# A hybrid encoder block on one core: x loaded and transposed in blocks of columns, and the norm's factors put into the gate results

## The chip, the cores and the metric

The kernel runs on one core of a Trainium2 chip. TensorE multiplies matrices, VectorE, ScalarE and GpSimd do elementwise work, SyncE issues most of the loads, and 16 DMA engines move the data between HBM and the core's memories. The metric is the device time of one execution in microseconds (us), less is better.

## What is computed

The reference, cut to the parts around the change (512 positions, 2048 channels, all in float32):

```python
def rms_norm(x, g):
    y = x * lax.rsqrt(jnp.mean(x * x, axis=-1, keepdims=True) + EPS)
    return y * g

def reference(x, c, w_ada, b_ada, norm_mix, w_in, ...):
    c_act = jax.nn.silu(c)
    mod = c_act @ w_ada[l] + b_ada[l]                      # 2048 -> 6 * 2048
    sh_m, sc_m, g_m, sh_f, sc_f, g_f = jnp.split(mod, 6, axis=-1)
    h = rms_norm(x, norm_mix[l]) * (1.0 + sc_m) + sh_m
    proj = h @ w_in[l]                                     # 2048 -> 512 + 1536 + 2048 + 2048
    y_s5 = s5_branch(proj[..., :512], ...)                 # two state-space scans, 32 groups
    y_fn = fnet_branch(proj[..., 512:2048])                # 2-D Fourier transform
    gate_s5 = jax.nn.sigmoid(proj[..., 2048:4096])
    gate_fn = jax.nn.sigmoid(proj[..., 4096:])
    merged = gate_s5 * (y_s5 @ w_branch_s5[l]) + gate_fn * (y_fn @ w_branch_fnet[l])
    x = x + g_m * (merged @ w_out[l])
    ...                                                    # a second norm, a SwiGLU layer, a last norm
```

## The kernel before

Every product is done with three matmuls: a weight is split into a rounded part `whi` (ScalarE, L123) and a rest `wlo` (VectorE, L124), the activations likewise into `hi` and `lo` (tiles `actA`, `actB`), and `mm3` (L206 to L208) sums three of the four products. Activations lie transposed: channel blocks k = 0 to 15 of 128 rows, 512 positions as columns.

The kernel is a list of steps. A step may have a job: a load (SyncE's queue), a preparation (the splits) and the matmuls that use it. `run_plan` walks the list: it issues loads in the order of the steps (moved forward by a job's `lead`) as long as buffers are free (five `raw`, eight `araw`, three `whi`/`wlo`), prepares up to three steps ahead, and then issues the step's own work. On TensorE and GpSimd the instructions stand in the order in which the program writes them; on VectorE and ScalarE a scheduler orders them, except that instructions marked `keep_in_program_order` stay in order among themselves. Each engine works through its own list in order.

The start needs `x` transposed (`xT`, the tile `mg`), the row factors of the norm (`rb`, from the sums of squares `xs`), and `mod[1]`, the scale, which is a product of `c` with 16.8 MB of `w_ada`. The scale comes in five blocks of 2, 4, 4, 4 and 2 channel blocks. The first is summed on TensorE (`ada_pe`, L312), the others by VectorE, one multiply-add per 128x512 piece (L283, L285, tiles `ada`), and a sum over partitions on TensorE (`ada_fin`, L329). `form_hs` then makes the scaled activations of a channel block: `s_mix` (L405), `htmp` = `xT` times `s_mix` times `rb` (L413), and its split. `start_w(k)` multiplies them with six gate tiles' weights, 18 matmuls for each k, and six accumulators stay open over k = 0 to 15.

Then six more gate tiles (n = 6 to 11) are computed, each from two weight halves, while the shift `mod[0]` (another 16.8 MB of `w_ada`) is summed in the same way. These twelve tiles are multiplied without the shift; they are stored as they are and finished later. In tile 11 `resplit` calls `form_h` behind each k: `htmp` is made again and the shift is added on the way into `hi` and `lo` (L127, L128). After its last k the pool that holds `xT` and `rb` is closed, and later tiles take its memory.

Next come `u_fn`, the 512 inputs of the S5 branch, and then 20 gate tiles, with hooks between their matmuls that build the S5 matrices in eight batches: the parameters (some 120 small operations on VectorE, recorded by `Deferred` and issued two at a time in tiles 6 to 10; they all show as L516), copies and transposes of them, loads of the tables `R` and `cn` (`s5_load`, L714 and L718) into memory that becomes free with the closed pools, `Y` on VectorE (`s5_a`, L731 to L736), and `TB` and `E` on GpSimd (L750 to L778), which TensorE transposes (L820). The rest (Fourier branch, output, SwiGLU layer) is some 2000 us of matmuls.

`sxT` is a copy of `xT` in HBM, read again much later; GpSimd issues its four stores (L935), the first instructions on its list behind the loads of S5 parameters.

## Time and profile before

| | us |
|---|---|
| median of 3 runs | 2518.16 (2514.17 to 2520.89) |
| the profiled execution | 2523.47 |
| its span, first to last instruction | 2521.7 |
| TensorE busy in the span | 2419.8 |
| VectorE busy | 1673.8 |
| ScalarE busy | 1014.5 |
| GpSimd busy | 562.4 |

The mean granted clock of TensorE is 0.977 of full speed. The span is 1.8 us shorter than the execution's own time. In the profile PE is TensorE, PEld its weight loads, DVE VectorE, ACT ScalarE, POOL GpSimd, SP SyncE, and a q behind the name is the engine's queue of DMA issues. A busy TensorE is not one at its peak, since its instructions are pipelined.

### The profile page before, as it was taken

To read this page: it belongs to the slowest core of one execution; us is meant where nothing else is said; L and a number is where in the kernel's file an instruction comes from. 1 tells how busy PE (TensorE), PEld (TensorE's weight loads), DVE (VectorE), ACT (ScalarE), POOL (GpSimd) and SP (SyncE) were. 2 spreads that over 40 slices of the span, in tenths; PEclk is the share of its full clock that TensorE was granted. 3 is DMA by queue.
4 is the path that set the end of the run, shared out by engine and by line. 5 is a ranking of instruction groups with operands and counts; after the bars stand their busy time and mean duration, and the time that the engine had idled before them with its cause. 6 is when DMAs were issued, how large, how long until landed. Compare 5 with 4: busy or idle time off the path is not lost.

```text
span 2521.7 us, 37777 instructions
## 1 busy us (share of the span) xinstructions
PE 2419.8 (96%) x14450; PEld 2147.8 (85%) x14450; DVE 1673.8 (66%) x2492; ACT 1014.5 (40%) x1420; POOL 562.4 (22%) x630
## 2 busy tenths in 40 slices
PE   6899899989999999999999999999999999999997
PEld 5787777778788888888999999999999978888886
DVE  6988677636666996668667676766667645554335
ACT  3224333333223432244555555555555522233223
POOL 1002999800002520000222222222222310010001
PEclk7899999989999999999999999999999999999998
DMA  9886645447774667763788888889888877754442
GB/s 367 287 298 129 158 137 157 140 136 242 232 238 146 199 194 234 243 218 107 174 197 193 193 200 190 199 201 197 195 197 194 213 273 244 239 167 163 148 142 90
DMA packets 440678, 496.33 MB, mean 197 GB/s; under 512 B 51104, under 2 KB 336288, under 8 KB 440496
## 3 DMA queue, kind: packets, MB, share of 16 engines
q1 hardware_dynamic: 359472, 384.68, 48.7%
q0 software_dynamic: 52736, 78.74, 17.5%
q10 hardware_dynamic: 28288, 30.49, 4.2%
q8 instruction: 113, 1.85, 0.3%
q14 instruction: 69, 0.57, 0.1%
HBM read 394.13 MB, written 40.89 MB: 173 GB/s over the span
## 4 chain that ended last, share of the span: by engine, by line
PE 73%; POOL 9%; DVE 7%; DMA 5%; issue 3%; ACT 1%; SPq 1%; ACTq 0%; DVEq 0%; POOLq 0%
PE ps_acc L206 7%; PE ps_acc L207 7%; PE ps_acc L208 7%; PE ps_acc L1498 6%; PE ps_acc L1497 6%; PE ps_acc L1499 6%; PE ps_acc L1666 3%; PE ps_acc L1667 3%; PE ps_acc L1665 3%; PE ps_accb L1499 3%; PE ps_accb L1498 3%; PE ps_accb L1497 3%; DMA raw<-in_w_in_dram 2%; DVE wlo L124 2%; PE ps_m L1499 1%
## 5 line engine op out<-in xcount | busy, mean ns | idle before, releaser
L124 DVE TENSOR_TENSOR wlo<-raw,whi 128x1024 fp32r<-128x1024 f32 (+2 forms) x264 | 323.3, 1225 | 151.5 <-ACT whi L123 144.7
L123 ACT CAST whi<-raw 128x1024 fp32r<-128x1024 f32 (+2 forms) x264 | 260.5, 988 | 401.3 <-PE ps_acc L207 180.5
L1451 POOL DMA_DIRECT2D wlo<-raw x160 | 192.3, 1202 | 895.6 <-ACT wlo L1450 569.9
L206 PE MATMUL ps_acc<-actB,whi 128*128 128x512 f32 x816 | 328.3, 402 | 0.0
L207 PE MATMUL ps_acc<-actB,whi 128*128 128x512 f32 x816 | 321.7, 394 | 0.0
L208 PE MATMUL ps_acc<-actB,wlo 128*128 128x512 f32 x816 | 321.3, 394 | 0.0
L124 DVE TENSOR_TENSOR lT<-raw,hT 128x1024 fp32r<-128x1024 f32 x160 | 195.5, 1222 | 133.7 <-ACT hT L123 133.5
L123 ACT CAST hT<-raw 128x1024 fp32r<-128x1024 f32 x160 | 167.6, 1047 | 161.6 <-issue 99.4
L124 DVE TENSOR_TENSOR actA<-ab,actA 128x512 fp32r<-128x512 f32 x88 | 61.7, 703 | 234.6 <-ACT actA L123 234.6
L1449 ACT CAST whi<-raw 128x768 fp32r<-128x768 f32 x160 | 133.2, 832 | 151.7 <-PE ps_acc L1498 144.7
L208 PEld LDWEIGHTS ps_acc<-actB,wlo 128*128 128x128 f32 x816 | 155.5, 191 | 33.8
L206 PEld LDWEIGHTS ps_acc<-actB,whi 128*128 128x128 f32 x816 | 156.3, 192 | 32.8 <-issue 2.5
L123 ACT CAST actA<-ab 128x512 fp32r<-128x512 f32 x88 | 54.7, 623 | 318.9 <-PE ps_m L1666 298.2
L207 PEld LDWEIGHTS ps_acc<-actB,whi 128*128 128x128 f32 x816 | 156.2, 191 | 30.1
L1460 DVE TENSOR_TENSOR raw<-raw 128x512 f32<-128x512 f32 x160 | 110.7, 692 | 71.0 <-DMA wlo<-raw 65.4
L1666 PE MATMUL ps_acc<-wlo,actA 128*128 128x512 f32 x352 | 137.3, 390 | 1.9 <-DVE wlo L124 1.9
L285 DVE SCALAR_TENSOR_TENSOR ada<-raw,c_s,ada 128x512 f32<-128x512 f32 x180 | 136.7, 759 | 3.4
L1665 PE MATMUL ps_acc<-whi,actA 128*128 128x512 f32 x352 | 137.6, 391 | 1.0 <-DVE ab L1509 0.9
L1667 PE MATMUL ps_acc<-whi,actA 128*128 128x512 f32 x352 | 137.0, 389 | 0.0
L1450 ACT ACTIVATE wlo<-raw 128x768 fp32r<-128x768 f32 x160 | 134.3, 840 | 0.0
L1688 POOL TENSOR_TENSOR actB<-actB 128x512 f32<-128x512 f32 x15 | 23.0, 1548 | 429.1 <-ACT fot L1686 429.1
L206 PE MATMUL ps_acc<-actA,whi 128*128 128x512 f32 x272 | 111.7, 411 | 2.4 <-ACT actA L123 2.4
(474 smaller groups left out, 7006.7 us busy)
## 6 DMA issues: line engine op xcount, KB each, us to landing
raw<-in_w_ffn_in_dram SPq DMA_DIRECT2D x168, 512.0 KB
raw<-in_w_ada_dram SPq DMA_DIRECT2D x128, 512.0 KB
wlo<-raw POOLq DMA_DIRECT2D x160, 384.0 KB, 5.6
raw<-in_w_in_dram SPq DMA_DIRECT2D x108, 512.0 KB
raw<-in_w_ffn_out_dram SPq DMA_DIRECT2D x88, 512.0 KB
araw<-in_w_ada_dram SPq DMA_DIRECT2D x64, 512.0 KB
ab<-sg SPq DMA_DIRECT2D x88, 256.0 KB
raw<-in_w_out_dram SPq DMA_DIRECT2D x32, 512.0 KB
```

What stands on the lines that cost most here:

```text
L123: A.copy(hi, src)
L124: V.tensor_tensor(out=lo, in0=src, in1=hi.bitcast(F32), op=ALU.subtract)
L206: PE.matmul(o, whi, ahi, start=start, stop=False)
L207: PE.matmul(o, whi, alo, start=False, stop=False)
L208: PE.matmul(o, wlo, ahi, start=False, stop=stop)
L1451: G.dma_start(out=lo, in_=r[:, :, 0:3], accum_op=ALU.add)
L1497: PE.matmul(o, wh[:, i, q], ah, start=first and opens, stop=False, skip_group_check=True)
L1498: PE.matmul(o, wh[:, i, q], al, start=False, stop=False, skip_group_check=True)
L1499: PE.matmul(o, wl[:, i, q], ah, start=False, stop=last, skip_group_check=True)
L1665: PE.matmul(o, gh[:, ts_], hi[:, cs], start=(k == 0), stop=False)
L1666: PE.matmul(o, gh[:, ts_], lo[:, cs], start=False, stop=False)
L1667: PE.matmul(o, gl[:, ts_], hi[:, cs], start=False, stop=(k == NF - 1))
```

## The change

- `x` is loaded in four blocks of 512 columns (all rows) instead of four blocks of rows, into `araw` buffers. The first block's load stands behind the loads of the scale's first block; the others stand among the scale's blocks 1 to 3. A block is transposed by TensorE through two `ps_m` banks, and ScalarE copies all of it to `xT` and sums the squares.
- The norm's factors are needed only later: `form_hs` takes `xT` times `s_mix` alone, `hi` in one ScalarE instruction and `lo` in one on VectorE. The results of the first twelve gate tiles are multiplied by `rb` on VectorE, where ScalarE copied them. `x_rstd` moves into the last scale block, and `rb` into another pool. `form_h` (tile 11) is as before.
- The second block of the scale stands behind both of the first gate steps, no longer ahead of the last of them.
- The S5 parameters and the four stores of `sxT` are kept in program order; the stores go to ScalarE's queue.

```diff
@@ constants, and the per-column vectors
-AHEAD = 1
...
-    pv = ps_m((P, P))
-    PE.transpose(pv, rows, ident)
-    V.tensor_copy(vec, pv)
+    def vec_columns():
+        pv = ps_m((P, P))
+        PE.transpose(pv, rows, ident)
+        V.tensor_copy(vec, pv)
@@ ada_pe: the first block of the scale
-    def ada_pe(width, then):
+    def ada_pe(width):
...
                 if q == parts - 1:
                     n = width // P
+                    vec_columns()
                     V.tensor_reduce(out=mod[1][:, 0:n], in_=pt[0], op=ALU.add, axis=mybir.AxisListType.X)
                     V.tensor_tensor(out=mod[1][:, 0:n], in0=mod[1][:, 0:n], in1=vec[:, KT:KT + n], op=ALU.add)
-                    then()
@@ the loads and transposes of x
-    xs_ = cpool.tile([P, 4, 4], F32, name="xs")
-    rb = y_pool.tile([P, S], F32, name="rb")
-
-    def x_job(t):
-        def load():
-            if t < 2:
-                r = [raw_tile([P, D // 2]) for _ in range(2)]
+    xs_ = cpool.tile([P, 7, 4], F32, name="xs")
+    rb = nat_pool.tile([P, S], F32, name="rb")
+
+    def x_step(j):
+
+        def load():
+            r = [y_pool.tile([P, 2, S], F32, tag="araw", bufs=ARAW_BUFS, name="xr") for _ in range(2)]
+            for h in range(2):
+                nc.sync.dma_start(out=r[h], in_=x[2 * h * P:2 * (h + 1) * P, j * S:(j + 1) * S].rearrange(
+                    "(t p) c -> p t c", p=P))
+            return r
+
+        def fn(r):
+            for i in range(4):
+                pt = ps_m((P, 4, P))
+                for t in range(4):
+                    PE.transpose(pt[:, t, :], r[t // 2][:, t % 2, i * P:(i + 1) * P], ident)
+                A.copy(mg[:, 4 * j + i, :], pt.rearrange("p t c -> p (t c)"))
+            if j:
+                squares(r)
             else:
...
-        def prep(r):
-            for q in range(4):
-                pt = ps_acc((P, 4, P))
-                for k in range(4):
-                    kk = (4 * q + k) % 8
-                    PE.transpose(pt[:, k, :], r[q // 2][:, kk * P:(kk + 1) * P], ident)
-                dst = mg[:, 4 * q:4 * q + 4, t * P:(t + 1) * P]
-                if q == 3:
-                    A.copy(dst, pt)
-                else:
-                    V.tensor_copy(dst, pt)
-            for h in range(2):
-                junk = ring.tile([P, D // 2], F32R, tag="whi", bufs=WH_BUFS, name="junk")
-                A.activation(out=junk, in_=r[h], func=AF.Square, accum_out=xs_[:, h, t:t + 1])
-            return None
-
-        return Job(load, prep, raw=(("raw" if t < 2 else "araw", 2),), keep=())
+                x0.append(r)
+
+        def squares(r):
+            for t in range(4):
+                junk = cpool.tile([P, S], F32, tag="tmp", bufs=3, name="junk")
+                tc.keep_in_program_order(A.activation(out=junk, in_=r[t // 2][:, t % 2, :], func=AF.Square,
+                                                      accum_out=xs_[:, j, t:t + 1]))
+
+        job = Job(load, lambda r: r, raw=(("araw", 2),), keep=(), hold=True)
+        if j == 0:
+            job.late = 2
+            return [(job, fn), (None, forms(*blocks[0])), (None, lambda _: squares(x0.pop()))]
+        return [(job, fn)]
...
@@ form_hs and gate_epi
         hi, lo = act_tile(k), act_tile(k)
-        split(hi, lo, scaled_x(k))
+        A.activation(out=hi, in_=mg[:, k, :], func=AF.Copy, scale=s_mix[:, k:k + 1])
+        V.scalar_tensor_tensor(out=lo, in0=mg[:, k, :], scalar=s_mix[:, k:k + 1], in1=hi.bitcast(F32),
+                               op0=ALU.mult, op1=ALU.subtract)
...
             if dst is sg5 and n < N_HS:
-                A.copy(s, pt)
+                V.tensor_tensor(out=s, in0=pt, in1=rb, op=ALU.mult)
@@ the steps of the start
-    start_steps = []
+    start_steps = ada_pe(blocks[0][1] * P) + x_step(0)
     for i, (k0, nk) in enumerate(blocks):
...
+        if i:
+            blk = ada_steps(1, k0 * P, nk * P, True, forms(k0, nk))
+            if i < 4:
+                blk[4:4] = x_step(i)
+            if i == 4:
+                blk.insert(1, (None, x_rstd))
+            at = len(start_steps) - (i > 1)
+            start_steps[at:at] = blk
         for k in range(k0, k0 + nk):
-            ws.append((wjob(w_in_v[:, k, G0:G0 + N_START * P]), start_w(k)))
-            ws[-1][0].lead = 3 + k - k0
-        if i == 0:
-            start_steps += [(x_job(t), nop) for t in range(4)]
-            start_steps += blk[:-1] + [(None, x_rstd)] + blk[-1:] + ws
-        else:
-            start_steps[-AHEAD:-AHEAD] = blk
-            start_steps += ws
+            start_steps.append((wjob(w_in_v[:, k, G0:G0 + N_START * P]), start_w(k)))
+            start_steps[-1][0].lead = (3 if i else 2) + k - k0
@@ Deferred.issue (the S5 parameters)
-                getattr(V, name)(*a, **kw)
+                tc.keep_in_program_order(getattr(V, name)(*a, **kw))
@@ gate tiles 7 to 10
-                nc.gpsimd.dma_start(out=sxT.rearrange("k p s -> p k s")[:, 4 * q:4 * q + 4],
-                                    in_=mg[:, 4 * q:4 * q + 4])
+                tc.keep_in_program_order(A.dma_start(
+                    out=sxT.rearrange("k p s -> p k s")[:, 4 * q:4 * q + 4], in_=mg[:, 4 * q:4 * q + 4]))
```

On SyncE's queue, at the head of the program (the columns are line, what is loaded from where, the shape, and how many in a row), before:

```order
L371 DMA raw<-in_x_dram 128x1024 x4
L371 DMA xr<-in_x_dram 128x1024 x4
L303 DMA araw<-in_w_ada_dram 128x4x256 x3
L136 DMA raw<-in_w_in_dram 128x768
L303 DMA araw<-in_w_ada_dram 128x4x256
L270 DMA araw<-in_w_ada_dram 128x2x512 x5
```

The same place in the changed kernel:

```order
L304 DMA araw<-in_w_ada_dram 128x4x256 x4
L370 DMA xr<-in_x_dram 128x2x512 x2
L135 DMA raw<-in_w_in_dram 128x768 x2
L271 DMA araw<-in_w_ada_dram 128x2x512 x4
L370 DMA xr<-in_x_dram 128x2x512 x2
```

Two loads of `x` instead of eight stand ahead of the first weights, and behind the scale's first block.

On VectorE, where tile 10 ends and the shift is added (`mod` is the shift of the last four channel blocks, `htmp` and `actA` are form_h's), before:

```order
L285 SCALAR_TENSOR_TENSOR ada<-araw,c_s,ada 128x512 x5
L124 TENSOR_TENSOR wlo<-raw,whi 128x1024
L285 SCALAR_TENSOR_TENSOR ada<-araw,c_s,ada 128x512
L124 TENSOR_TENSOR wlo<-raw,whi 128x1024
L330 TENSOR_TENSOR mod_91<-ps_m,vec 128x4
L413 SCALAR_TENSOR_TENSOR htmp<-xT,s_mix,rb 128x512
```

The same place in the changed kernel:

```order
L457 TENSOR_TENSOR sg<-ps_acc,rb 128x512
L528 CAST t_1061<-kj 64x64
L123 TENSOR_TENSOR wlo<-raw,whi 128x1024
L528 TENSOR_SCALAR t_1061<-t_1061 64x64
L331 TENSOR_TENSOR mod_88<-ps_m,vec 128x4
L528 TENSOR_TENSOR si<-si,t_1061 64x64
L528 TENSOR_SCALAR t_1062<-t_1060 64x64
L429 SCALAR_TENSOR_TENSOR htmp<-xT,s_mix,rb 128x512
L528 TENSOR_TENSOR t_1061<-t_1061,t_1062 64x64
```

The S5 parameters (L528, before L516) now reach into the sixteen `htmp`, 35 of the 123 behind the first of them; all were done ahead of these before.

On ScalarE's list, gate tiles 6 to 8 of the changed kernel (`sg` is a gate tile's result, `whi` a weight's rounded part):

```order
L122 CAST whi<-raw 128x1024
L947 DMA sxT<-xT 128x4x512
L460 DMA sg_100<-sg 128x512 x3
L122 CAST whi<-raw 128x1024 x2
L947 DMA sxT<-xT 128x4x512
```

The stores of `sxT` stand between the weights' conversions, where before GpSimd issued all four with no work ahead of them. From the first `TB` on GpSimd's list is the same in both kernels, and so are TensorE's and ScalarE's from the first table of that batch on.

## Rows read from the trace of the kernel before

**Rows 1.** Stretch: busy us of PE, PEld, DVE, ACT, POOL; clock, DMA share, GB/s.

```profile
238.00:478.00 240.00, 218.22 (x1121) 176.22 (x1119) 171.82 (x214) 79.96 (x150) 225.48 (x334) 0.96 0.54 151
478.00:2521.00 2043.00, 1994.73 (x12404) 1800.83 (x12404) 1306.88 (x1848) 856.35 (x1146) 329.09 (x280) 0.99 0.71 193
```

**Rows 2.** Who waited for whom up to 490 us: us in total, times, longest.

```profile
PE ps_m L329 <- DVE ada L285: 19.8, 4, 12.0
...
PE ps_m L820 <- POOL TB L752: 15.0, 8, 4.6
...
POOL TB L750 <- DVE Y L733: 22.4, 1, 22.4
...
SPq L714 <- DVE htmp L413: 9.5, 1, 9.5
```

**Rows 3.** The chain that ended last, 200 to 240 us: start, us, what.

```profile
204.78 0.23 PE ps_acc L206
...
212.09 1.41 DVE htmp L413 x2
...
230.77 5.32 DMA R<-in_s_b_re_dram
...
237.35 1.10 DVE Y L736
```

**Rows 4.** Busy time by stretch of the start (columns as in rows 1).

```profile
0.00:20.00 20.00, 11.90 (x85) 11.59 (x85) 10.14 (x29) 12.81 (x23) 5.98 (x15) 1.00 0.92 318
20.00:60.00 40.00, 24.79 (x104) 21.06 (x104) 29.63 (x85) 8.37 (x13) 0.68 (x1) 0.66 1.04 400
60.00:100.00 40.00, 35.89 (x153) 29.33 (x152) 38.39 (x82) 9.88 (x14) 0.00 (x0) 0.91 0.74 244
100.00:160.00 60.00, 56.29 (x245) 46.37 (x244) 57.21 (x135) 18.05 (x29) 0.00 (x0) 0.94 1.02 341
160.00:180.00 20.00, 20.00 (x98) 16.87 (x97) 18.85 (x34) 5.10 (x6) 0.00 (x0) 1.00 0.92 305
...
sum 214.00, PE 182.86 PEld 151.09 DVE 180.12 ACT 71.69 POOL 6.66; mean PE 26.12 PEld 21.58 DVE 25.73 ACT 10.24 POOL 0.95
```

**Rows 5.** Instructions in order of time: start, us, engine, line [idle before, releaser].

```profile
0.72 2.08 SPq L371 DMA_DIRECT2D raw<-in_x_dram  x4
...
17.64 3.04 POOL L935 DMA_DIRECT2D sxT<-xT  x4 [12.99 <-DVE xT L384]
...
50.66 1.87 PE L329 MATMUL ps_m<-ones,ada 128*128 128x1 f32 x8 [11.96 <-DVE ada L285]
...
190.50 0.74 DVE L413 SCALAR_TENSOR_TENSOR htmp<-xT,s_mix,rb 128x512 f32<-128x512 f32 x1
...
237.00 1.29 POOL L750 TENSOR_TENSOR TB<-Y,powr 128x512 f32<-128x512 f32 x1 [22.36 <-DVE Y L733]
```

**Rows 6.** DMA issues up to 214 us: count, size of each, us to landing.

```profile
sxT<-xT POOLq DMA_DIRECT2D x4, 1024.0 KB, 14.5
...
raw<-in_x_dram SPq DMA_DIRECT2D x4, 512.0 KB
```

**Rows 7.** Groups of instructions: count, busy us, mean ns, idle before.

```profile
L413 DVE SCALAR_TENSOR_TENSOR htmp<-xT,s_mix,rb 128x512 f32<-128x512 f32 x32 | 22.9, 746 | 0.0
...
L384 DVE COPY xT<-ps_acc 128x512 f32<-128x512 f32 x12 | 7.7, 687 | 1.7 <-PE ps_acc L379 1.7
...
L387 ACT ACTIVATE junk<-xr 128x1024 fp32r<-128x1024 f32 x4 | 4.2, 1054 | 0.0
```

**Rows 8.** VectorE's busy time in L516 alone, by stretch.

```profile
0.00:60.00 60.00, 6.90 (x42) 0.77 1.00 373
60.00:180.00 120.00, 14.07 (x81) 0.94 0.91 303
```

**Rows 9.** TensorE's busy time and granted clock around its first gate matmuls.

```profile
30.79:36.89 6.10, 5.22 (x11) 0.50 1.03 415
36.89:38.70 1.81, 1.81 (x8) 0.99 1.03 404
```

More of the change, by code (lines that the diff above doesn't have):

```diff
@@ L392, in x_rstd, with forms, fn @@
+        return [(job, fn)]
+    x0 = []
+    def forms(k0, nk):
+        def fn(_=None):
+            for k in range(k0, k0 + nk):
+                form_hs(k)
+        return fn
     def x_rstd(_):
-        v, r, t = (xs_[:, i, :] for i in (2, 3, 1))
-        V.tensor_tensor(out=v, in0=xs_[:, 0, :], in1=xs_[:, 1, :], op=ALU.add)
+        v, r, t = (xs_[:, i, :] for i in (4, 5, 6))
+        V.tensor_reduce(out=v, in_=xs_[:, 0:4, :].rearrange("p j t -> p t j"), op=ALU.add, axis=mybir.AxisListType.X)
@@ L447, in encoder_block @@
     blocks = [(0, 2), (2, 4), (6, 4), (10, 4), (14, 2)]
-    start_steps = []
+    start_steps = ada_pe(blocks[0][1] * P) + x_step(0)
     for i, (k0, nk) in enumerate(blocks):
-        def then(k0=k0, nk=nk):
-            for k in range(k0, k0 + nk):
-                form_hs(k)
-        blk = ada_pe(nk * P, then) if i == 0 else ada_steps(1, k0 * P, nk * P, True, then)
-        ws = []
-        for k in range(k0, k0 + nk):
-            ws.append((wjob(w_in_v[:, k, G0:G0 + N_START * P]), start_w(k)))
-            ws[-1][0].lead = 3 + k - k0
-        if i == 0:
-            start_steps += [(x_job(t), nop) for t in range(4)]
-            start_steps += blk[:-1] + [(None, x_rstd)] + blk[-1:] + ws
-        else:
-            start_steps[-AHEAD:-AHEAD] = blk
-            start_steps += ws
+        if i:
[6 more added lines that the diff above has]
+            start_steps[at:at] = blk
+        for k in range(k0, k0 + nk):
+            start_steps.append((wjob(w_in_v[:, k, G0:G0 + N_START * P]), start_w(k)))
+            start_steps[-1][0].lead = (3 if i else 2) + k - k0
     steps.extend(start_steps)
```

4 lines of the change are left out of this document (removed).

## The prediction

> **What bounds the kernel now.** I read the stages first (busy time of each engine in stretches of the span), then who waited for whom, then the chain of work that ended last, then the start instruction by instruction.
>
> The stages split the span in three. From 478 us on TensorE is busy 1994.7 of 2043 us, and the change moves nothing there. From 238 to 478 us GpSimd is busy 225.5 of 240 us [rows 1]: it builds the eight S5 batches one after the other, and TensorE waits for it eight times, 15.0 us in all. GpSimd itself waited once, 22.4 us at the head, for the first `Y` of VectorE [rows 2]. So this stretch is a block of fixed length, and the end is set by when it begins. The chain shows what sets that: the last two `htmp` end at 212.09 + 1.41 = 213.5 us [rows 3]. They are the last readers of `xT` and `rb`, whose memory the S5 tables `R` take; SyncE's queue sat 9.5 us for them [rows 2]. `R` lands at 230.77 + 5.32 = 236.1 us, `Y` follows [rows 3], and GpSimd begins at 237.0 [rows 5].
>
> So the question is how early the last `htmp` can end. Before it VectorE is the fullest engine: busy 180.1 of 214 us, and from 60 to 160 us idle for only 4.4. The DMA engines are full from 20 to 60 us and from 100 to 160 us (share 1.04 and 1.02) [rows 4]. TensorE waited 19.8 us for the `ada` sums [rows 2], 12.0 of them at 50.66 us [rows 5]. Three resources run close to each other here, and the time is that of the latest.
>
> **The change, part by part.**
>
> *Order of the loads.* Before, SyncE's queue begins with all of `x` (eight loads of 512 KB), and GpSimd adds the store of `sxT` (4 x 1024 KB) at 17.64 us, as soon as `xT` is whole [rows 5, 6]. Now the first gate matmul needs four loads of `w_ada` (2.1 MB), a quarter of `x` (1.05) and two weight rows (0.79). At the 318 GB/s of the first 20 us [rows 4] that is 12.4 us; with the conversions about 16 us. The sum of the second block needs 9.9 MB. At the 400 GB/s of 20 to 60 us [rows 4], after some 3 us, they are there at 28 us and the sum at 30, against 50.66 before [rows 5].
>
> 400 GB/s held for 40 us [rows 4]. The Trainium skill, *DMA: Bandwidth & Descriptors*, section "Where 436 GB/s comes from", has HBM bind at about 358 GB/s for a core; by it those 9.9 MB take 27.7 us, not 24.8. The trace disagrees with it, and the sum goes by the trace.
>
> *VectorE's work up to the last `htmp`.* Two `htmp` in a row take 1.41 us [rows 3], so one costs 0.66 us behind another. Taken away: 16 `htmp` of `form_hs`, 10.6 us (the scale now sits in ScalarE's copy and in VectorE's subtraction), and 12 copies of `xT`, mean 0.687 us [rows 7], some 0.63 behind one another, 7.6 us, which go to ScalarE. Added: the product of a gate tile with `rb`, 11 of the 12 ahead of the last `htmp`. No row shows a product that reads PSUM; the copy from PSUM bounds it below (0.63), the three-operand form above (0.75 [rows 7]). I take 0.66, nearest to the copy since it is one pass over the same 512 columns: 7.3 us, between 6.9 and 8.3. The subtraction becomes a three-operand form, 0.06 us more each, 1 us. Sum: 180.1 - 0.5 (cut at 213.5) - 10.6 - 7.6 + 7.3 + 1.0 = 169.7 us. The S5 parameters (L516, 123 small operations, 21.0 us busy, 0.17 each [rows 8]) are as many as before, but 35 of them now stand between the `htmp`, where before none did.
>
> *VectorE's idle time* was 33.9 us of 214 [rows 4]. Now it idles 11.5 us of the first 13, until weights arrive, then has 14 us of work up to 30 us: 3 us idle. From there I give it the idle share of 60 to 160 us, 4.4%. The `htmp` stretch holds 27 us of work (16 `htmp` and 14 sums into `actA`/`actB` at 0.66, 35 small ones at 0.17, one `wlo` of 1.1), so 142.7 lie ahead of it. Less the 15.5 done by 30 us, that is 127; over 0.956, 133. VectorE can begin the `htmp` at 163 us, where before they began at 190.50 [rows 5].
>
> *DMA.* Up to the last `w_ada` load of the shift 56 MB must move, the store of `sxT` included: it now stands on ScalarE's queue in gate tiles 7 to 10. 27.3 MB up to the last scale block at 400 GB/s are 68 us, the other 28.8 MB at the 341 GB/s of 100 to 160 us [rows 4] 84 us, after 3 us: 155 us at the earliest, 157 with the last sum. Issuing the four stores cost GpSimd 3.04 us [rows 5]; on ScalarE it lies beside weight conversions that run three ahead, and costs at most those 3 us where that cover is gone.
>
> *TensorE.* At full clock a matmul takes 0.23 us [rows 3], a gate step of 18 of them 4.1. ScalarE evacuates the second block's transposes and squares its `x` ahead of the third step's conversions: four copies and four squares, the squares at most 1.05 us each, the time of those twice as wide [rows 7]. TensorE waits for this once, 6 us at most; later blocks have a step between. From 16 us: two steps, half of them at half clock (11 us), that wait, 14 steps (57), 48 transposes and four sums (9): the gate start ends near 99 us. Five tiles of 48 matmuls and one sum, 12 us each, follow: 159 us.
>
> The latest is VectorE with 163, the others come at 157 and 159. Where three run so close, each delays the others; I add 3 us: 166. The `htmp` took 213.5 - 190.5 = 23.0 us; with 35 small operations among them it is 28 to 29. So the last `htmp` ends at 194.5, **19 us earlier**. From there to GpSimd's first product the same loads and waits stand (213.5 to 237.0, 23.5 us [rows 3, 5]): it begins at 218. TensorE's own way into the S5 stretch gains some 17 us and has its 15 us of waits as slack. The stretch and all behind it come 19 us earlier.
>
> The profiled execution took 2523.5 us, 5.3 above the median of 2518.2. Off the one, 19 us leave 2504.5; off the median, **2499 us**, 0.8% less. What a measurement of this kernel can tell from no change is about 0.3%, 7.5 us.
>
> **Rivals.**
>
> *More.* If the three do not disturb each other and VectorE's early idle shrinks to 12 us, the `htmp` begin at 160 and end at 188: 25.5 us, 2492.5. For it: from 100 to 160 us VectorE idled only 2.8 us while TensorE and DMA were full too [rows 4]. Against it: the start has four block sums, and at each VectorE hands over to TensorE and waits.
>
> *TensorE stays at half clock.* Its first 6 us of gate matmuls ran at 0.50, the next at 0.99 [rows 9]; over 20 to 60 us, behind the 12 us wait, the granted clock was 0.66 [rows 4]. If the waits of the new start hold it at half for five more steps, each costs 18 x 0.20 = 3.6 us more, 18 us: tile 11 begins at 178, the last `htmp` ends at 206, and 7 us are left: 2511. Against it: the wait shrinks from 12 us to 6 and the steps behind it are dense. The Trainium skill, *TensorE: Matmul & The Clock Gate*, section "HAM oscillation — how this bites in real kernels", says that a TensorE that waits between bursts begins each burst throttled; by that rule this case is the likely one wherever waits remain, and the row of 20 to 60 us agrees.
>
> *Slower: the loads wait for buffers.* `x` now holds two of the eight `araw` buffers until ScalarE has squared it, SyncE's queue is in order, and every later load stands behind that wait; the 4.2 MB of `sxT` come on top in the tiles. From 60 to 100 us, where loads waited for buffers, DMA moved 244 GB/s [rows 4]. The last `htmp` comes later than 213.5 when the shift's last load lands after 184, a mean under 56 MB / 181 us = 309 GB/s. At 290 it lands at 196, and the last `htmp` ends at 225: 11.5 us late, 2530. Against it: the mean over the first 180 us was 326 GB/s with that slow stretch in it [rows 4], and VectorE's work for a block of four columns falls from 5.0 to 2.6 us beside its 14 us of sums and weights.
>
> *Nothing gained.* `R` is loaded behind gate weights in SyncE's queue, which wait for TensorE's pace; if that sets it, GpSimd begins no earlier than TensorE allows. 2514 to 2518. Against it: TensorE comes 17 us earlier too.
>
> **How the numbers follow.** Forecast (2494 to 2507): 0.62. More (2488 to 2494): 0.13. Half clock (2507 to 2513): 0.12. Nothing gained: 0.07. Slower: 0.06. The likeliest gives 2499. The range from 2489 to 2511 holds the forecast and most of its two neighbours, 0.82; it takes in the bounds of the product with `rb` (1.4 us) and of the stores' issue (3 us). Faster by over 0.3% is under 2510.6: 0.62 + 0.13 + 0.08 of the half clock's 0.12 = 0.83. Within 0.3%: the other 0.04 and 0.07, 0.11. Slower: 0.06.
>
> **What would show it.** In the changed profile: the first gate matmul at 16 us; the second block's sum near 30; the first `htmp` at 163 to 168, the last at 192 to 197; GpSimd's first product at 216 to 221; TensorE's wait for `ada` under 10 us instead of 19.8; DMA at 340 GB/s or more from 20 to 140 us; GpSimd's stretch as long as before. It is wrong if the last `htmp` ends after 206, if the clock stays below 0.7 past 50 us, or if GpSimd's stretch grows.

## The result, and the profile after

The change made the kernel slower: 2535.01 us (median of six runs, 2527.36 to 2542.55) against 2518.94 for the kernel before, a ratio of 1.0076 with a 95% interval of 1.0060 to 1.0092. Forecast were 2499 us, and 2489 to 2511 as the range. Beside the runs of e6 to e8 the changed kernel was measured again: 2533.8 us, 1.0066 (1.0043 to 1.0088). Its times lie in two groups, 2517 to 2530 and 2539 to 2543, about half of them in each; the kernel before has one group (2509 to 2523). The profiled execution after took 2529.40 us (its span is 2527.6), so it is of the lower group.

Stretches of the start after the change (the columns are those of [rows 4]: length, busy us of PE, PEld, DVE, ACT, POOL, clock, DMA share, GB/s):

```profile
0.00:20.00 20.00, 14.50 (x68) 14.53 (x69) 1.10 (x8) 1.50 (x2) 3.63 (x11) 1.00 0.92 314
20.00:60.00 40.00, 26.03 (x94) 20.14 (x93) 26.52 (x44) 16.77 (x36) 0.00 (x0) 0.79 0.82 286
60.00:100.00 40.00, 37.56 (x180) 30.82 (x179) 31.06 (x56) 21.11 (x41) 0.00 (x0) 0.96 0.89 303
100.00:160.00 60.00, 59.66 (x276) 49.30 (x276) 55.41 (x126) 12.16 (x14) 0.00 (x0) 1.00 0.95 328
160.00:180.00 20.00, 16.04 (x63) 12.95 (x62) 17.18 (x47) 3.15 (x3) 0.00 (x0) 0.83 1.09 363
...
0.00:221.47 221.47, 190.67 (x832) 155.28 (x832) 170.33 (x380) 75.58 (x136) 3.63 (x11) 0.93 0.81 277
0.00:100.00 100.00, 78.09 (x338) 65.49 (x339) 58.68 (x107) 39.38 (x78) 3.63 (x11) 0.90 0.87 298
```

VectorE was busy 58.7 of the first 100 us; before it was 78.2. From 20 to 60 us the DMA engines moved 286 GB/s instead of 400 [rows 4], and from 160 to 180 us, where TensorE had been full, it now has a gap of 4 us and a lower clock.

The milestones, each from the timeline of its engine (start, us, engine, line, idle before and releaser in brackets):

```profile
5.50 13.78 PE L313 MATMUL ps_accb<-c_s,araw 128*128 128x1 f32 x64 [5.50 <-DMA araw<-in_w_ada_dram]
19.15 0.46 PE L227 MATMUL ps_m<-ident,rows 128*128 128x128 f32 x1
19.39 3.71 PE L378 MATMUL ps_m<-ident,xr 128*128 128x128 f32 x16
25.13 0.80 PE L205 MATMUL ps_acc<-actA,whi 128*128 128x512 f32 x1 [2.03 <-ACT actA L422]
```

```profile
192.77 0.74 DVE L429 SCALAR_TENSOR_TENSOR htmp<-xT,s_mix,rb 128x512 f32<-128x512 f32 x1
...
220.07 1.41 DVE L429 SCALAR_TENSOR_TENSOR htmp<-xT,s_mix,rb 128x512 f32<-128x512 f32 x2
```

```profile
243.75 1.28 POOL L762 TENSOR_TENSOR TB<-Y,powr 128x512 f32<-128x512 f32 x1 [21.42 <-DVE Y L745]
```

So the gate matmuls begin at 25.1 us (before 30.8 [rows 9]), but the first `htmp` comes at 192.8 (before 190.5 [rows 5]), the last ends at 221.5 (before 213.5 [rows 3]) and GpSimd begins its S5 batches at 243.8 (before 237.0 [rows 5]): 6.8 us late, where the span is 5.9 us longer. The lead of the start was lost on the way, and more.

Who waited, after (us in total, times, longest). The first block is up to 490 us, the second is SyncE's queue up to 240 us:

```profile
POOL TB L762 <- DVE Y L745: 21.4, 1, 21.4
...
PE ps_m L330 <- DVE ada L286: 11.5, 3, 9.7
```

```profile
SPq L271 <- DMA sxT<-xT: 8.4, 1, 8.4
...
SPq L271 <- ACT junk L388: 6.6, 4, 4.2
```

GpSimd waited once at its head, as before [rows 2], and TensorE waited less for `ada` than before (11.5 us instead of 19.8). New are two of SyncE's waits: for a store of `sxT` and for ScalarE's squares (`junk`).

### The profile page after: what moved, and what is told of

It reads as the page before. It is cut to its first block, busy times and chain, and to the rows that moved or that the text cites. A ratio compares the mean times of both kernels' runs of the same rounds, so it can differ in the third digit from the quotient of the medians.

```text
span 2527.6 us, 37762 instructions
## 1 busy us (share of the span) xinstructions
PE 2426.8 (96%) x14450; PEld 2152.5 (85%) x14450; DVE 1668.3 (66%) x2476; ACT 1016.8 (40%) x1436; POOL 561.4 (22%) x626
## 4 chain that ended last, share of the span: by engine, by line
PE 74%; POOL 9%; DVE 7%; DMA 5%; issue 3%; ACT 1%; SPq 0%; ACTq 0%; DVEq 0%; POOLq 0%
PE ps_acc L205 6%; PE ps_acc L207 6%; PE ps_acc L206 6%; PE ps_acc L1510 6%; PE ps_acc L1511 6%; PE ps_acc L1509 6%; PE ps_acc L1678 3%; PE ps_acc L1679 3%; PE ps_acc L1677 3%; PE ps_accb L1511 3%; PE ps_accb L1509 3%; PE ps_accb L1510 3%; DMA raw<-in_w_in_dram 3%; DVE ada L286 2%; DVE wlo L123 2%
```

## The experiments

Each was measured beside the kernel before on the same chip. Four times tell where a kernel stands: the last matmul of the gate start (`wlo` of its sixth tile), the first `htmp` (the column "tiles 6-10" is the difference of the two), the start of the last `htmp`, and GpSimd's first `TB`. Each is read from the timeline of the run's profile; the time is a median.

| kernel | gate start | tiles 6-10 | first htmp | last htmp | first TB | time | ratio, 95% interval |
|---|---|---|---|---|---|---|---|
| before | 132.1 | 58.4 | 190.5 | 212.8 | 237.0 | 2515-2519 | 1 |
| changed | 124.5 | 68.2 | 192.8 | 220.7 | 243.8 | 2535.0 | 1.0060 to 1.0092 |
| e1 S5 free | 125.1 | 67.2 | 192.3 | 214.5 | 238.8 | 2520.4 | 1.0004 to 1.0027 |
| e2 stores early | 121.3 | 62.5 | 183.8 | 211.8 | 234.7 | 2519.6 | 1.0003 to 1.0033 |
| e3 both back | 128.2 | 58.4 | 186.6 | 208.9 | 232.5 | 2512.7 | 0.9977 to 1.0001 |
| e4 x0 in raw | 121.3 | 68.6 | 189.9 | 217.8 | 240.3 | 2527.3 | 1.0028 to 1.0066 |
| e6 factors only | 121.2 | 58.4 | 179.5 | 201.8 | 225.7 | 2506.5 | 0.9944 to 0.9975 |
| e7 e3, x1 early | 126.7 | 58.4 | 185.1 | 207.4 | 231.7 | 2510.3 | 0.9962 to 0.9984 |
| e8 changed, x1 early | 119.9 | 68.7 | 188.6 | 216.5 | 240.4 | 2534.4 | 1.0035 to 1.0086 |
| e9 before, stores late | 128.9 | 58.4 | 187.3 | 209.5 | 233.2 | 2514.6 | 0.9985 to 1.0006 |
| e10 before, S5 in order | 131.5 | 63.6 | 195.1 | 215.7 | 241.3 | 2519.3 | 0.9995 to 1.0022 |
| e11 changed, wrev late | 123.4 | 68.1 | 191.5 | 219.4 | 241.9 | 2530.0 | 1.0040 to 1.0080 |
| e12 e6, wrev late | 121.8 | 58.3 | 180.1 | 202.4 | 226.3 | 2511.9 | 0.9968 to 0.9990 |
| e13 e6, stores late | 118.3 | 68.1 | 186.4 | 208.7 | 232.8 | 2513.1 | 0.9982 to 1.0001 |
| e14 before, copies on ACT | 131.7 | 58.4 | 190.1 | 212.3 | 237.1 | 2518.9 | 1.0003 to 1.0023 |
| e15 e1, more sg buffers | 125.5 | 66.0 | 191.5 | 213.8 | 237.3 | 2518.3 | 1.0002 to 1.0021 |

Where TensorE has no gap and VectorE is ready for the first `htmp`, the tiles take 58.4 us. The executions of one kernel spread, too: four more profiles of the changed kernel (e5, e16 to e18) have the gate start at 121.0 to 124.5, tiles of 68.3 to 69.0 and the last `htmp` at 217.5 to 220.8, so 3 us of a milestone from a single profile mean little.

**Undoing the two moves (e1 to e3).** e1 takes the order away from the S5 parameters, e2 gives the stores back to GpSimd, e3 does both:

```diff
-                tc.keep_in_program_order(getattr(V, name)(*a, **kw))
+                getattr(V, name)(*a, **kw)
...
-                tc.keep_in_program_order(A.dma_start(
-                    out=sxT.rearrange("k p s -> p k s")[:, 4 * q:4 * q + 4], in_=mg[:, 4 * q:4 * q + 4]))
+                nc.gpsimd.dma_start(out=sxT.rearrange("k p s -> p k s")[:, 4 * q:4 * q + 4],
+                                    in_=mg[:, 4 * q:4 * q + 4])
```

> The changed kernel with one edit undone: the S5 parameters (L528) are not kept in program order; the scheduler puts all 123 ahead of the last block sum of the scale, none of them among the twelve gate tiles. Theory VectorE (the small operations, 14 us of them behind the gate start, fill VectorE in tiles 6 to 10, 60.8 us busy of 67.9, and stand among the htmp): tiles 6 to 10 take 59 to 61 us instead of 67.9, the htmp stretch 23 to 24 instead of 28.6; the last htmp ends near 209 instead of 221.4, and the time is 2517. Theory DMA (the stores of sxT make the gate weights late): the tiles still take 66 to 68 us and only the htmp stretch shortens, by 5 us; last htmp at 216, 2524. Theory start (nothing behind the start counts): no change, 2529.

> The changed kernel with one edit undone: the four stores of sxT go back to GpSimd's queue, where they start when xT is whole (near 95 us). Theory DMA: the gate weights of tiles 6 to 10 are no longer late, VectorE's order notwithstanding; tiles 6 to 10 take 60 to 62 us instead of 67.9, the htmp stretch stays at 28 to 29; last htmp at 214, 2522. Theory VectorE: tiles 66 us or more, 2527 to 2529. Against both: from 95 us the stores meet the scale's last loads, and the gate start ends 2 to 4 us later than 124.8.

> The changed kernel with both edits undone (S5 parameters placed by the scheduler, stores of sxT on GpSimd's queue): what is left of the change is the order of the x loads and the norm's factors in the gate results. Theory VectorE and theory DMA together: tiles 6 to 10 take 58 to 59 us as before, the htmp stretch 23, so the 7.6 us lead of the gate start (124.8 against 132.3) is kept: last htmp at 206, 7 us earlier than before the change, 2511 to 2513. Theory start (the tiles lose the lead whatever stands in them, since they wait for the loads): last htmp at 213 or later, 2518 or more. If VectorE alone counts, this equals e1; if DMA alone counts, e2 less 5 us.

Both theories hold for a part each. In e1 the last stretch (first to last `htmp`) falls from 27.9 to 22.3 us and the tiles stay at 67, as theory DMA has them. In e2 the tiles take 62.5 us and the stretch 28.0; its gate start did not end later, as expected, but at 121.3. In e3 they take 58.4 and 22.3, as before the change. Together the two moves cost the last `htmp` 9 to 12 us (217.5 to 220.8 against 208.9). In time, on this one chip, e1 is 7.8 us and e2 6.9 us longer than e3. What is left of the change, e3, is 0.1% faster than before, with an interval that holds 1.

**One part alone, in the kernel before (e6, e9, e10, e13).** e6 puts only the factors into the gate results (`form_hs` and `gate_epi` of the change, `rb` in the other pool); e9 only moves the stores, e10 only keeps the S5 order, e13 is e6 with the stores moved.

> The kernel before with one part of the change alone: form_hs without rb, rb multiplied into the results of gate tiles 0 to 11 on VectorE (rb in the other pool). Loads of x, S5 parameters and stores as before. VectorE loses 16 htmp (10.6 us) up to the last block of the scale and gets 12 products (7.3 to 8 us) from gate tile 0 on. Theory VectorE (it sets the pace from 60 to 160 us): the gate start ends 5 to 8 us earlier than 132.3, and with the stores out of the way the lead is kept: last htmp at 206 to 208 instead of 213.5, 2510. Theory DMA or start (loads set the pace of the gate start): its end moves by under 3 us, 2514 to 2516.

> The kernel before with one part of the change alone: the four stores of sxT on ScalarE's queue in gate tiles 7 to 10, kept in order. Theory DMA: tiles 6 to 10, 58.2 us before (132.3 to 190.5), take 64 to 67 us since 4.2 MB more stand against the shift's loads; the gate start, free of them, ends 2 to 4 us earlier; last htmp at 217 to 219 instead of 213.5, time 4 to 6 us longer, 2520. If the stores cost nothing where ScalarE issues them: last htmp at 210 to 213, 2514.

> The kernel before with one part of the change alone: the S5 parameters kept in program order, so that none runs before gate tile 6. Theory VectorE: 14 us of small operations (before in VectorE's gaps of the first 60 us and around the last block sum) fill the tiles and some stand among the htmp: tiles 6 to 10 take 59 to 62 us instead of 58.2, the htmp stretch 25 to 28 instead of 23; last htmp at 217 to 221, 2520 to 2523. If VectorE has room in the tiles (50.4 us busy of 60.1): 2515 to 2517.

> e6 (factors in the gate results, x loaded as before, S5 parameters placed by the scheduler) with the four stores of sxT on ScalarE's queue in gate tiles 7 to 10. If the late stores cost tile time because VectorE's products wait for the gate results' stores, which stand behind sxT in ScalarE's queue (3.6 to 3.8 us at 126 us in the changed kernel and e1): tiles 6 to 10 take 64 to 67 us instead of 58.1, last htmp at 207 to 210, 2511 to 2513. If they cost it because SyncE's loads wait for these stores (8.4 us at 126 us in the changed kernel, 8.7 in e1, none in e9), which hangs on which load comes eight issues behind which store: anything from 58 to 67 us, and the profile shows SyncE waiting for sxT where the tiles are long and not where they are short.

e6 is the best kernel of all, 0.41% faster than before (0.25 to 0.56%): the factors alone bring the last `htmp` 11.0 us forward. Its start stretches, and what VectorE does in the first 20 us of it:

```profile
0.00:20.00 20.00, 11.59 (x85) 11.29 (x85) 9.98 (x28) 12.72 (x23) 5.89 (x14) 1.00 0.92 315
20.00:60.00 40.00, 25.07 (x104) 21.36 (x104) 29.85 (x98) 9.05 (x13) 0.76 (x2) 0.62 1.04 400
60.00:100.00 40.00, 38.81 (x172) 31.92 (x172) 37.30 (x87) 11.84 (x16) 0.00 (x0) 0.96 0.88 302
```

```profile
9.75 0.69 DVE L384 COPY xT<-ps_acc 128x512 f32<-128x512 f32 x1 [0.56 <-PE ps_acc L379]
...
12.07 0.14 DVE L518 TENSOR_SCALAR t<-ls 64x1 f32<-64x1 f32 x1
...
13.07 5.55 DVE L384 COPY xT<-ps_acc 128x512 f32<-128x512 f32 x9 [0.69 <-PE ps_acc L379]
```

VectorE is busy 77.1 of the first 100 us, the DMA engines are full from 20 to 60 us. Set against e3 (the factors and the new start), the new order of `x`, with ScalarE's copies and the later second block that belong to it, costs 7.1 us of last `htmp`, all of it in the gate start (128.2 against 121.2). Before the change the stores could go late for nothing (e9, 0.9985 to 1.0006; this speaks against theory DMA as I had put it), but with the factors in they cost 9.7 us of tile time (e13 against e6), as in the changed kernel. The S5 order alone makes the first `htmp` 5.2 us later against the gate start, and the last one 2.9 (e10); in time that is not told from nothing. These 5.2 us are not TensorE's, which has no gap there and has already begun tile 11 (296 matmuls up to the first `htmp`; in e9, with 58.4 us, 275):

```profile
131.50:195.10 63.60, 63.52 (x296) 52.84 (x295) 58.38 (x180) 16.51 (x25) 0.00 (x0) 1.00 0.89 290
```

It is VectorE that comes late to the `htmp`, behind the S5 parameters, and the `htmp` stretch is then shorter (20.6 us), not longer as expected.

**Why the late stores cost what they cost (e15).** Two readings were open: VectorE's product waits for a buffer whose store stands behind `sxT` in ScalarE's queue (4.2 us at 126 to 131 us in the changed kernel), or SyncE's loads wait for `sxT`. e15 gives tiles 0 and 1 buffers of their own:

```diff
-            s = cpool.tile([P, S], F32, tag="tmp", bufs=3, name="sg")
             if dst is sg5 and n < N_HS:
+                s = (nat_pool.tile([P, S], F32, tag="sgt", bufs=2, name="sg") if n < 2 else
+                     cpool.tile([P, S], F32, tag="tmp", bufs=3, name="sg"))
```

> e1 (the changed kernel with the S5 parameters placed by the scheduler) with two more buffers for the results of gate tiles 0 and 1, so that VectorE's product of tile 3 no longer waits for the store of tile 0's result behind a store of sxT. Theory products: VectorE's wait of 3.6 us at 126 us goes, its sums go on, tiles 6 to 10 take 62 us or less instead of 67; last htmp at 209 to 211, 2516. Theory SyncE (the loads wait 8.7 us for the store of sxT all the same): tiles 65 us or more, last htmp at 213 to 216, 2519 to 2521.

VectorE's wait for these stores falls from 4.1 us in e1 to 1.0, and the tiles still take 66.0 us: the products' buffers are not the cause. SyncE's waits for transfers, 60 to 195 us, in e13 and in e15:

```profile
SPq L270 <- DMA sxT<-xT: 11.5, 2, 9.3
```

```profile
SPq L271 <- DMA sg<-sg: 7.9, 3, 6.2
...
SPq L271 <- DMA sxT<-xT: 3.4, 2, 2.7
```

In the compiled instruction list a DMA issue waits for one of eight semaphores (`DMAHW0` to `DMAHW7`) that an earlier transfer used, whichever queue that was on. Of the changed kernel, two lines of ScalarE's list and two of SyncE's:

```
L947 DMA sxT<-xT 128x4x512 [waits DMAHW7_49]
L460 DMA sg_100<-sg 128x512 [waits DMAHW2_49,DVE_49]
L271 DMA araw<-in_w_ada_dram 128x2x512 [waits DMAHW7_49,DVE_49]
L271 DMA araw<-in_w_ada_dram 128x2x512 [waits DMAHW2_49,DMAHW0_49,DVE_49]
```

The trace bears this out: the store of `sxT` that ScalarE issued at 124.8 us landed at 134.52, and SyncE's next load on its semaphore was issued at 135.11. So a load can stand behind a 1 MB store of another engine. But in e15 that wait is 3.4 us in all and the tiles are hardly shorter. The other candidate is plain DMA time. With late stores the engines' DMA share from 124 to 180 us is 1.02 to 1.06 (0.94 to 1.01 with early ones), and the issue of the shift's last load ends later: at 165.9 us in e13 against 159.1 in e6, 171.5 in e1 against 165.9 in e3, 166.0 in e9 against 164.8 before.

What this costs TensorE can be seen in e13: it waits once, for the third of the shift's four block sums, and its clock is 0.50 from there to 170 us. In e9, where the gate start ends 10.6 us later, it has no gap (first line the wait, then the tiles of e13 and of e9):

```profile
165.18 1.84 PE L329 MATMUL ps_m<-ones,ada 128*128 128x1 f32 x8 [6.24 <-DVE ada L285]
...
118.30:186.40 68.10, 61.82 (x275) 51.03 (x274) 54.89 (x105) 12.12 (x15) 0.00 (x0) 0.92 0.98 337
...
128.90:187.30 58.40, 58.40 (x275) 48.98 (x274) 48.86 (x118) 16.00 (x25) 0.00 (x0) 1.00 1.02 361
```

The same sum is waited for in the changed kernel (4.0 us), e1 (6.3), e4 (4.3), e8 (4.1), e11 (4.4), e15 (4.1) and e17 (3.1), all with late stores; with early ones e2 waits 1.7 us for it, e3, e6 and e7 not at all. So by these profiles late stores cost TensorE time where it comes early enough to wait for this sum. With them the first `htmp` never comes before 186 us; with early stores it comes at 179.5 (e6) and 183.8 (e2). The two ends of e13 and e9 (186.4 and 187.3) would fit a fixed floor under it, but the changed kernel does not: its gate start ends between 119.9 (e8) and 124.5 us, and the tiles keep 68.0 to 69.0 us. How much of the cost is SyncE's wait and how much the bytes was not separated.

**The start (e4, e7, e8).** e4 loads the first block of `x` into two `raw` buffers, so that its squares no longer hold `araw`; e7 (on top of e3) and e8 (on top of the changed kernel) also move the second block's step between the first two gate steps:

```diff
-            if i < 4:
+            if i == 1:
+                start_steps[-1:-1] = x_step(i)
+            elif i < 4:
                 blk[4:4] = x_step(i)
```

> The changed kernel with one edit: the first block of x is loaded into two of the five raw buffers instead of two of the eight araw buffers, so that the loads of the scale's second block don't wait for its squares. Theory start (that wait, SyncE idle until 26.94 us, makes the second block's sum late): the next w_ada load is issued at 20 to 21 us instead of 26.94, the first sum behind the two gate steps runs at 42 to 45 us instead of 48.9 (if ScalarE's copies and squares of the next x block hold the conversions instead: 47 to 49), and the gate start ends 4 to 6 us earlier than 124.8, near 120. By theories VectorE and DMA most of this is lost again in tiles 6 to 10, first htmp at 190 to 193, 2526 to 2529; by theory start it is kept, first htmp at 187, 2523 to 2525.

> e3 (S5 parameters placed by the scheduler, stores of sxT on GpSimd) with x's first block in raw buffers, as in e4, and the step of its second block moved between the first two gate steps. e4 showed SyncE's queue free at 16 us and yet the second block's sum at 48.1: ScalarE copied and squared the second x block, which TensorE transposes behind both gate steps, ahead of the next three weight conversions, and VectorE waited for these from 36 to 42 us. Theory ScalarE's order: the conversions run at 32 to 37 us, the sum at 41 to 43, the gate start ends at 118 to 120; the tiles follow with 60 to 62 us: last htmp at 202 to 204, 2506 to 2508. Theory DMA (the loads behind set the pace of the tiles): the start gains 6 us but the first htmp still comes at 184 to 187, last at 207 to 209, 2511 to 2513.

> The changed kernel with the start of e7 alone (x's first block in raw buffers, second block's step between the first two gate steps); S5 parameters kept in program order and stores of sxT on ScalarE's queue, as in the changed kernel. Theory ScalarE's order: the second block's sum at 41 to 43 us, gate start ends at 117 to 119. Theories DMA and VectorE: the tiles, which take 67.9 us in the changed kernel, take 71 to 74 here, first htmp at 190 to 192, last at 218 to 220, 2526 to 2529: the gain of the start is lost behind it. If instead the tiles keep 68 us: first htmp at 186, last at 214, 2523.

In e4 the next load of `w_ada` is issued at 16.43 us instead of 26.94, and the second block's sum runs at 48.1 (47.6 to 49.1 in the changed kernel's profiles): the buffers that the first block of `x` holds were not what made it late. ScalarE's list made it late (changed kernel, ScalarE and then VectorE):

```profile
37.44 1.07 ACT L379 COPY xT<-ps_m 128x512 f32<-128x512 f32 x2 [9.30 <-PE ps_m L378]
38.77 1.07 ACT L379 COPY xT<-ps_m 128x512 f32<-128x512 f32 x2 [0.26 <-PE ps_m L378]
39.74 0.63 ACT L388 ACTIVATE junk<-xr 128x512 f32<-128x512 f32 x1
...
42.20 2.28 ACT L122 CAST whi<-raw 128x768 fp32r<-128x768 f32 x3
```

```profile
27.08 8.62 DVE L286 SCALAR_TENSOR_TENSOR ada<-araw,c_s,ada 128x512 f32<-128x512 f32 x11
43.05 0.96 DVE L123 TENSOR_TENSOR wlo<-raw,whi 128x768 fp32r<-128x768 f32 x1 [7.34 <-ACT whi L122]
```

ScalarE sat idle for 9.3 us until TensorE, behind both gate steps, transposed the next block, then copied and squared it, and only then converted three weights that had long been there; VectorE's sums stood behind the first of these. With that moved, the sum runs at 42.1 us in e8 and at 45.1 in e7. But e8's tiles take 68.7 us and its time is that of the changed kernel; in e7 the gate start gains 1.5 us where 8 to 10 were expected. The middle of the start is paced by something else (in e7 VectorE is busy 35.7 of 40 us from 60 to 100 us); what, was not settled.

**The copies (e14).** All copies of `xT` go to ScalarE in the kernel before:

```diff
-                if q == 3:
-                    A.copy(dst, pt)
-                else:
-                    V.tensor_copy(dst, pt)
+                A.copy(dst, pt)
```

> The kernel before with the twelve copies of xT that VectorE makes given to ScalarE, nothing else. The prediction's sum takes 7.6 us off VectorE's work ahead of the htmp for this. Theory prediction: last htmp at 206 to 208 instead of 213.5. Theory gap (they ran in the first 20 us, while VectorE had nothing else to do, so taking them away only widens the gap): last htmp at 212 to 216, 2514 to 2518.

Theory gap: last `htmp` at 212.3 against 212.8. The 7.6 us of copies were worth 0.5 us, and by its time the kernel is if anything slower (1.0003 to 1.0023). Its first gate matmul runs at 42.3 us, 11 us later than before, and its gate start ends as before: 11 us of the first matmul were worth nothing here either.

**The two groups of times (e4, e5, e11, e12, e16 to e18).** e4's profile happened to be of the upper group. e11 and e12 move GpSimd's six loads of `wrev` behind the S5 batches (in the changed kernel and in e6):

```diff
-        hook(90 + 36 * g, rev_rows, g)
+        hook(300 + 14 * g, rev_rows, g)
```

> The changed kernel as it is, on the chip of the next runs. All theories: 1.006 to 1.009 times the kernel before, about 2530. Its earlier times fall in two groups 13 us apart (2527 to 2529, 2541 to 2543); the profile of e4 shows one set of eight stores M (ScalarE's queue, 381 us) that took 14.4 us instead of 5.2 to 6.3 and cost GpSimd's stretch 13 us. If such a stall makes the upper group, a profile of it shows a set of M over 12 us; a profile of the lower group shows none.

> The changed kernel with GpSimd's six loads of wrev (1 MB each, between the S5 batches) moved behind the last batch. If the upper group of its times (2539 to 2543 of 2522 to 2543) comes from stores M on ScalarE's queue that fall behind such a load (in e4: load issued at 378.9, stores at 381.2 for 14.4 us): no set of M takes over 7 us, the times form one group, and GpSimd's stretch is up to 6.9 us shorter (six issues of 1.15 us), so 2516 to 2523. If the group has another cause, half of the times stay above 2532. In both cases the last htmp stays at 221.

> e6 (the norm's factors in the gate results, all else as before) with the same move of the six wrev loads. GpSimd's stretch, 236 us in every run so far but e4, loses up to 6.9 us of issues; 6 MB then move from 460 to 500 us beside the gate weights. If GpSimd sets that stretch: 2500 to 2503. If the burst delays gate weights behind it, or TensorE's own order sets the stretch: 2506 to 2510.

> The changed kernel as it is, one more profile. Its times lie in two groups, 2522 to 2530 and 2539 to 2543. If this profile is of the upper group, it shows where the 13 us are: by the theory of e4, a set of stores M of over 12 us between two S5 batches and GpSimd's first-to-last TB at 249 us or more instead of 236.5 to 237.2. If it is of the lower group, no set of M over 7 us.

> The changed kernel as it is. If this profile is of the upper group (over 2535 us): by the theory of e4 one set of stores M between two S5 batches takes over 12 us, and GpSimd's first-to-last TB is 249 us or more instead of 236 to 238. If the 13 us are elsewhere (before the first TB, or behind the last), the theory falls.

> As e17, one more profile of the changed kernel. In the upper group: a set of M over 12 us and 249 us or more from GpSimd's first to its last TB; in the lower: no set over 7 us and 236 to 238 us.

e17 took 2538.9 us, e18 2517.3. The other profiles of the changed kernel, all of the lower group, have no set of stores `M` over 6.5 us. In e17, the fourth set of stores `M` on ScalarE's queue, the load of `wrev` that GpSimd issued before it, and GpSimd's waits:

```profile
381.50 14.54 ACTq L858 DMA_DIRECT2D M<-KF  x8
```

```profile
379.17 1.14 POOL L1012 DMA_DIRECT2D wrev<-in_w_branch_fnet_dram  x1
```

```profile
POOL D L790 <- DVE w L880: 26.1, 4, 18.9
POOL TB L762 <- DVE Y L745: 20.5, 1, 20.5
```

In e18 the set comes first and its issue takes 5.2 us; the load is issued 12 us behind it:

```profile
369.84 5.24 ACTq L858 DMA_DIRECT2D M<-KF  x8
```

```profile
381.72 1.14 POOL L1012 DMA_DIRECT2D wrev<-in_w_branch_fnet_dram  x1
```

What stalls is not the small stores but their issue, and the trace has the reason: it is the shared semaphores again. The seventh store of e17's set uses the semaphore of a weight load that SyncE issued at 380.33 us, 1.2 us behind the `wrev` load. Twelve of this load's sixteen parts had landed by 385.7 us; the last four came at 394.4 to 394.8, and the store was issued at 394.81. In e4 it was the same: a weight load issued at 380.05 landed at 394.39, and the set's next store came at 394.41. In e18 the weight load ahead of the set was issued at 368.0 us and had landed whole by 371.9.

From the first batch's first `TB` to the last batch's e17 takes 251.1 us and e18 236.9, though e17 began 1.1 us earlier. So 13 of the 21.6 us between the two are made in the S5 stretch, and both profiles of that height (e4 with 2535.5 us, e17) show the same stalled set behind a `wrev` load. The other 8.5 us lie behind it, where profiles of the lower group differ as much (from the start of the last batch to the end 2039.6 us in e18, 2049.1 in the profile after). e11 fits, with a reserve: none of its sets is over 6 us, and its times lie within 2528 to 2536, but they are only five, and the median is 2530, not 2516 to 2523 as expected. Six loads in one burst probably cost something later: e12, forecast at 2500 to 2510, takes 5.4 us more than e6, with GpSimd's stretch 3.1 us shorter. What decides between the groups within one kernel is not settled; the runs part between the first and the second batch.

## Why the prediction was wrong, step by step

**What sets the end: right, with one gap.** The last `htmp`, then `R`, `Y` and GpSimd: 8.0 us later at the one, 6.8 at the other. In e1 to e15 the first `TB` follows the last `htmp` by 22 to 26 us. But "a block of fixed length" failed: from the first to the last batch it takes 233 to 238 us in all profiles but two, and 250.2 and 251.1 in e4 and e17. If every time of the upper group has this, it is some half of the changed kernel's executions, and it lifts the measured median; the lower group alone is slower than before too (2517 to 2530 against 2509 to 2523).

**VectorE's work: right.** 169.7 us forecast up to the last `htmp`, 170.33 measured. The product with `rb` takes 0.68 us alone and 1.88 for three in a row (0.66 forecast), the `htmp` stretch 28.7 (28 to 29 forecast).

**VectorE's idle time: this is the step that failed.** The sum gave it 11.5 + 3 us up to 30 us and 4.4% from there, 17.6 of the first 100 us. It was idle for 41.3 of them. Add these 23.7 us to the 166 forecast for the first `htmp`: 189.7; measured 192.8. That says where the time went, and the experiments say by what. The last `htmp` ended at 221.5 instead of 194.5. By single profiles, of these 27 us 12 are the two moves (209.6 in e3), 7 the new order of `x` (202.6 in e6), and by 8 the factors alone already stay behind the forecast. Three things in the sum were wrong. The first two have one reason, that a sum over 214 us does not say when the work can be done.

- The copies of `xT` were taken off at 7.6 us. They run in the first 20 us (in e6 from 9.75 to 18.6), when VectorE has nothing else; e14 shows what they were worth: 0.5 us.
- The S5 parameters were counted "as many as before", and only the 35 among the `htmp` were priced. But 42 of them had run in the first 60 us [rows 8], in gaps; kept in order they all stand behind the gate start. With the stores early this costs 4.1 us up to the first `htmp` and 5.7 in the last stretch, of which the gate start, rid of them, gives back 6.9 (e2 against e3): 2.9 us net, as in e10, which is no more than two profiles of one kernel can differ by.
- The first gate matmul was forecast at 16 us from its loads (12.4 us) and conversions. It came at 25.1: TensorE's 64 pieces of the first block ran until 19.3 us, then come transposes, copies and conversions in a row. The second block's sum came at 48.9 instead of 30, in large part behind ScalarE's list (42.1 in e8, where that is moved). "TensorE waits for this once, 6 us at most" was 9.7.

**TensorE: wrong with it.** The gate start ended at 124.8 instead of 99, the tiles took 68.2 us instead of 60. What paces the gate start between the second block's sum and its end stays open (e7, e8).

**DMA: wrong in two terms.** "At the 400 GB/s of 20 to 60 us" was the rate of a stretch in which the DMA engines were never short of transfers (share 1.04 [rows 4]). In the changed kernel SyncE's queue stood for buffers again and again (from 19.7 to 26.9 us it issued nothing), the share was 0.82 and the rate 286. The Trainium skill's limit of about 358 GB/s (*DMA: Bandwidth & Descriptors*, "Where 436 GB/s comes from"), which the prediction set against its rate, is not what bound here: e6 again holds 400 from 20 to 60 us, the kernel before 393 from 40 to 60, when the stores of `sxT` had landed, and the changed kernel 363 from 160 to 180. And the price of the moved stores was only their issue, at most 3 us, beside their 4.2 MB in the sum of bytes. Early, in a stretch where the DMA engines are just as full (1.04 from 20 to 60 us), they cost the gate start 2.9 us (e6 against e13); late, they cost 9.7 us of tiles as soon as TensorE came earlier.

**The rivals.** "Slower: the loads wait for buffers", given 0.06, names the right outcome, 2530, and half of the mechanism: the stores in the tiles and loads that cannot run ahead. But its own condition was not met: the shift's last load landed at 176.6 us, not after 184, and the mean up to then was 315 GB/s, not under 309, so that the right outcome is in part luck. And the wait that it names, the buffers held by `x`, is worth under 1 us for the first block (e4); for the later blocks it was not tested. "TensorE stays at half clock" did not come as described: the clock was 0.50 from 42 to 59 us, as it was before from 44 to 57, and 0.96 from 60 to 100. A lower clock shows in the tiles, once: TensorE waits 4 us for the third shift sum,

```profile
169.67 1.83 PE L330 MATMUL ps_m<-ones,ada 128*128 128x1 f32 x8 [3.96 <-DVE t L528]
```

and from 169.6 to 175 us the granted clock is 0.50, over 160 to 180 us 0.83, where before, without a wait, it was 1.00 [rows 4]. That agrees with the Trainium skill (*TensorE: Matmul & The Clock Gate*, "HAM oscillation — how this bites in real kernels"), where a TensorE that waits between bursts of matmuls begins the next one throttled.

**The part that would have been right.** The factors in the gate results alone (e6) gain 0.41%, with VectorE's 16 saved `htmp` in the stretch where it is full. Forecast for the whole change were 0.8%.

## What to carry to other kernels

Price removed work by the stretch it stood in: work that an engine did in a gap is worth nothing when it goes, and work that could fill a gap costs its full time when an order pins it behind the gap. Split a change of several parts in thought and look for the part whose stretch is bound by what it removes; here only the factors were worth having. Price a store that is moved later by who waits for the loads around it at its new place, and do so with the rest of the change come forward: the same move was free in the kernel before (e9) and cost 9.7 us of tiles beside the factors (e13).

## What the runs showed that was not expected

A load on SyncE's queue waited 8.4 us (9.3 in e13) for a 1 MB store that ScalarE had issued, through one of eight shared semaphores. The issue of eight 32 KB stores took 14.5 us instead of 5.2 in the same way: a weight load issued 1.2 us behind a 1 MB load on GpSimd's queue took 14.5 us to land, instead of 3.9 in e18, and a store needed its semaphore. This 9 us delay grew to 14 us in the S5 stretch (e17). And five profiles of one kernel place the same `htmp` 3.3 us apart (217.5 to 220.8), so a single profile cannot judge a step of that size.
